# A transformer layer on one core: the last product turned to tokens on the partitions, and the first half's outputs queued behind the last casts

## The chip, the core and the metric

The kernel runs on one core of a Trainium2 chip. Its engines are TensorE (PE, matmuls into the accumulation memory PSUM, with the weight loads shown as PEld), VectorE (DVE), ScalarE (ACT), GpSimd (POOL) and SyncE (SP, which here only issues DMA transfers). Each engine works through its own queue in order, and waits there for results of the others. The metric is the device time of one execution in microseconds (us); a table further down says how the profile's span stands to it.

## What is computed

One layer of a diffusion backbone over 1024 tokens of 1024 features: two attention mixers, then a feed-forward part. Only the end of the layer matters here:

```python
u = h @ w_up                                  # 1024 x 5632
u = conv(u, 3 taps along the tokens) + conv_b
gate, val = jnp.split(u, 2, axis=-1)
y = (jax.nn.silu(gate) * val) @ w_down        # 1024 x 2816 by 2816 x 1024
x = _layer_norm(ALPHA * x + gate2 * y, ln2_g, ln2_b)
```

`gate2` is one number for each feature. The LayerNorm takes the mean and the variance over the 1024 features of a token, and `ln2_g`, `ln2_b` are again one number for each feature. All is in 32-bit floats.

## The kernel before

**Layout.** Until the last stage the features are on the partitions: eight feature tiles f of 128 rows, with the tokens along the free dimension. The tokens are cut into two halves of 512 (h0, h1), and for the last LayerNorm the second half into two quarters (`LN2_S`, line 43: 0 to 512, 512 to 768, 768 to 1024). A scale that is one number for each feature is then one number for each partition, which an instruction takes as a scalar operand.

**Split matmuls.** Each operand is split into a high and a low half (`split`, lines 80 to 87: a cast on ACT gives `hd`, then a subtraction on DVE, line 87, gives `ld`), and a product is three matmuls, high by high, high by low, low by high (`mm3`, lines 89 to 92). So a k-tile of a product can start on PE with `hd` alone and stops at its second matmul where `ld` is not there yet.

**The down projection.** It is done by Strassen's scheme with seven products of half size. In the code's order they are 1, 6, 2, 7, 4, 5 (the loop over `p` at line 1503) and then product 3, which is the last one. Each of the six has 11 k-tiles, with four feature tiles of 512 tokens: 12 matmuls of 512 columns for a k-tile (`product`, line 1465). `dload` (line 1213) loads the two operands of a k-tile by two transfers on SP's queue (lines 1220 and 1221) and splits them; it is called up to three k-tiles ahead (`dnext`), into a ring of four slots (`ring`, line 1150). The operands of product 3 are loaded during products 7, 4 and 5 for the first seven k-tiles (`D3AT`, line 49, each at a fixed place), and behind product 5 for the other four. The results of a product are added onto the residual `zz` by DVE (`accum`, line 1436) while the next product runs.

**Order of the instructions.** The order on PE is the order of the code (line 1177). On the other engines and on SP the scheduler of the framework sets a fixed order when the kernel is built, from readiness and from the order in the code. Work that is to run beside a product is put on a list `pend` with distances; `tick` (line 1004) counts the matmul columns that were issued and emits the next step when its distance is reached, and `drain` emits what is left.

**LayerNorm with features on the partitions** (`ln_steps`, line 1018). Sums and sums of squares over the features come from matmuls with a vector of ones (`stats`), the reciprocal root from a power on POOL (line 1038), diagonal matrices (`diags`) and matmuls with a matrix of ones spread mean and scale over the partitions (`cast`, line 1045), and ACT copies them to `rb` and `mb` (line 1050). Then, for each of the eight feature tiles, `apply` multiplies by `rb` on DVE (line 1055), subtracts `mb` (line 1057, on POOL for all tiles of the first half, on DVE and POOL in turn for the second quarter) and calls `emit2`: an affine function on ACT with the feature's gain and bias (line 1430) and the output's transfer on SP (line 1431). The first half goes this way during product 5, by the distances `LN2_D`.

**Product 3** works on the second half's 512 tokens and gives feature tiles 0 to 3; feature tiles 4 to 7 are complete after product 5. It is done for the third quarter of the tokens first (`r = LN2_S[1]`): matmuls of 256 columns, seven k-tiles for all four feature tiles, then the other four k-tiles for each. The quarter's LayerNorm by `ln_steps`, with the distances `LN2_E`, runs during the product of the last quarter, which has the same form: 4 feature tiles x 11 k-tiles x 3 matmuls of 256 columns.

**The last 256 tokens** are normalized the other way round. `tok(f)` (line 1555) transposes feature tile f of both 128-token tiles by PE into PSUM (`zt`, line 1559), so that tokens are on the partitions and the statistics over the features are one `bn_stats` per 512 features (line 1562). Tiles 4 to 7 are transposed during the product of the third quarter, and tiles 0 to 3 each after its product of the last quarter has been added (`accum`), the last of them after PE's last product. Then DVE subtracts the mean and multiplies by the gain (line 1617), and multiplies by the reciprocal root and adds the bias (line 1607; for the first token tile ACT and POOL do this, lines 1604 and 1605). Four transfers of 256 KB take the result out (line 1610).

Of the kernel before, what the change touches and what calls it, by code (L numbers as in the profile page):

```python
# [13 lines left out]
P = 128  # L14
# [25 lines left out]
LN2_E = 3500.0, 3000.0, 1500.0, 800.0, 500.0  # L40
# [11 lines left out]
OTP = (0, 0), (0, 1)  # L52
OTO = (0, 0), (0, 1), (1, 0), (1, 1)
OTK = 4
OTA = 1
OTB = 2
# [13 lines left out]
def layer_kernel(  # L70
# [8 lines left out]

    def split(src, hi, lo, hi_eng, lo_eng):  # L80
        if hi_eng is nc.scalar:
            nc.scalar.copy(hi, src)  # L82
# [4 lines left out]
        lo_eng.tensor_tensor(out=lo, in0=src, in1=hi.bitcast(F32), op=ALU.subtract)  # L87
# [930 lines left out]
    def ln_steps(zs, zq, s, nm, emit, first, gap, gap1, gap2, each, pm=2, order=range(KT)):  # L1018
# [34 lines left out]
        def apply(f):  # L1053
# [6 lines left out]
        return [(first, stats), (gap, diags), (gap1, cast)] + [(gap2 if n == 0 else each, lambda f=f: apply(f))  # L1060
                                                for n, f in enumerate(order)]
# [400 lines left out]
    d3, evict, after = [], [], []  # L1462
    h0, h1 = hsl(0), hsl(1)

    def product(p):
# [3 lines left out]
        for k in range(NH):  # L1469
# [8 lines left out]
            h, l = dq.pop(0)  # L1478
            for f in range(4):
# [23 lines left out]
    for p in (1, 6, 2, 7, 4, 5):  # L1503
        if p == 6:
# [4 lines left out]
            for a in (0, 1):  # L1509
                nc.sync.dma_start(lnr[a], ln2_row[a].partition_broadcast(P))  # L1510
        if p == 5:
# [35 lines left out]

    s = LN2_S[-1]
    w = s.stop - s.start
    nt = w // P  # L1550
# [4 lines left out]
    def tok(f):  # L1555
        if f % 4 == 0:
            zt[f // 4] = [sml(f"zt{f}_{t}", keep=True) for t in range(nt)]
        for t in range(nt):
            nc.tensor.transpose(zt[f // 4][t][:, (f % 4) * P:(f % 4 + 1) * P],
                                zv(f, slice(s.start + t * P, s.start + (t + 1) * P)), ident)  # L1560
            if f % 4 == 3:
                nc.vector.bn_stats(out=bst[:, t, f // 4], in_=zt[f // 4][t])

    todo = [4, 5, 6, 7]
# [13 lines left out]
    for f in range(4):  # L1578
# [3 lines left out]
        tok(todo.pop(0))  # L1582
    pend += ln_steps(zs2, zq2, r, "b1", emit2, *LN2_E, LN2_P[1])
    r = LN2_S[2]
    for f in range(4):
        o = sml(f"yl{f}_{r.start}")[:, 0:r.stop - r.start]
        last_mm(o, f, r, range(NH))
        accum(f, r, o, True)
        if todo:
            tok(todo.pop(0))  # L1590
        todo.append(f)
    hput(*[f"{a}d3_{k}" for k in range(len(D3AT)) for a in "hl"])
    hfree += xs
    tok(3)
    for t in range(nt):
        nc.vector.bn_aggr(out=mv[:, t], in_=bst[:, t].rearrange("p a b -> p (a b)"))
    nc.vector.tensor_scalar(out=mv[:, :, 1], in0=mv[:, :, 1], scalar1=LN_EPS, scalar2=None, op0=ALU.add)
    nc.gpsimd.tensor_tensor(out=mv[:, :, 1], in0=mv[:, :, 1], in1=mhalf[:, 0:nt], op=ALU.pow)
    ot = {}

    def last(t, a):
        o = ot[t, a]
        if (t, a) in OTP:
            nc.scalar.activation(o, o, AF.Identity, scale=mv[:, t, 1:2])
            nc.gpsimd.tensor_tensor(out=o, in0=o, in1=lnr[1][:, a], op=ALU.add)
        else:
            nc.vector.scalar_tensor_tensor(out=o, in0=o, scalar=mv[:, t, 1:2], in1=lnr[1][:, a],
                                           op0=ALU.mult, op1=ALU.add)
        ts = slice(s.start + t * P, s.start + (t + 1) * P)
        nc.sync.dma_start(out[4 * a:4 * a + 4, :, ts].rearrange("f p q -> p f q"),  # L1610
                          o.rearrange("p (f q) -> p f q", q=P))

    drain(OTK)
    for n in OTO:
        t, a = n
# [123 lines left out]
```

## Time and profile before

| what | us |
|---|---|
| median of three runs | 1586.05 |
| lowest and highest of them | 1584.53, 1586.13 |
| the profiled execution, whole | 1583.75 |
| its span, first to last instruction | 1582.0 |
| PE busy in the span | 1526.0 (96%) |
| DVE busy | 1192.4 (75%) |
| ACT busy | 811.3 (51%) |
| POOL busy | 759.6 (48%) |

All places in time below are microseconds from the span's start in the profiled execution. A row of an engine's timeline gives the start, the duration over all instructions of the row, the engine, the line of the code, the operation, what it writes and reads, the shapes and their number; in brackets stands how long the engine was idle before it and what ended that. A row of a group gives after the bar the busy time and the mean of one in nanoseconds. The mean clock that TensorE was granted over the whole span is 0.995 of full speed.

### The profile page before, as it was taken

To read this page: it belongs to the slowest core of one execution; us is meant where nothing else is said; L and a number is where in the kernel's file an instruction comes from. 1 tells how busy PE (TensorE), PEld (TensorE's weight loads), DVE (VectorE), ACT (ScalarE), POOL (GpSimd) and SP (SyncE) were. 2 spreads that over 40 slices of the span, in tenths; PEclk is the share of its full clock that TensorE was granted. 3 is DMA by queue.
4 is the path that set the end of the run, shared out by engine and by line. 5 is a ranking of instruction groups with operands and counts; after the bars stand their busy time and mean duration, and the time that the engine had idled before them with its cause. 6 is when DMAs were issued, how large, how long until landed. Compare 5 with 4: busy or idle time off the path is not lost.

```text
span 1582.0 us, 22065 instructions
## 1 busy us (share of the span) xinstructions
PE 1526.0 (96%) x7680; PEld 1266.0 (80%) x7680; DVE 1192.4 (75%) x1758; ACT 811.3 (51%) x1441; POOL 759.6 (48%) x738
## 2 busy tenths in 40 slices
PE   6999999999999999999999999999999999999996
PEld 5878788878886887777788898888888888888876
DVE  7797646628887777788674779888888787657885
ACT  5422222448887667688522565444444444435642
POOL 0583302426667556665432554766667664021142
PEclk9999999999999999999999999999999999999998
DMA  9695662322236555532451122333334447996721
GB/s 378 231 321 183 207 214 83 120 81 66 63 99 162 139 126 139 115 84 41 142 174 66 67 95 91 109 107 115 111 107 120 110 113 189 365 267 209 257 94 54
DMA packets 112367, 229.98 MB, mean 145 GB/s; under 512 B 12960, under 2 KB 27808, under 8 KB 112160
## 3 DMA queue, kind: packets, MB, share of 16 engines
q1 hardware_dynamic: 96816, 198.93, 37.9%
q0 software_dynamic: 10400, 20.19, 8.3%
q10 hardware_dynamic: 5040, 9.46, 1.6%
q8 instruction: 60, 0.98, 0.3%
q14 instruction: 51, 0.42, 0.1%
HBM read 177.35 MB, written 65.86 MB: 154 GB/s over the span
## 4 chain that ended last, share of the span: by engine, by line
PE 79%; DVE 9%; ACT 4%; DMA 4%; issue 3%; POOL 2%; SPq 0%; DVEq 0%; ACTq 0%; POOLq 0%
PE ptr L531 5%; PE p L91 4%; PE p L92 4%; PE p L90 4%; PE b L92 3%; PE b L91 3%; PE b L90 3%; PE a L91 2%; PE d L91 2%; PE c L91 2%; PE d L90 2%; PE c L90 2%; PE a L90 2%; PE c L92 2%; PE d L92 2%
## 5 line engine op out<-in xcount | busy, mean ns | idle before, releaser
L541 DVE TENSOR_TENSOR ptl<-ptr,pth 128x512 fp32r<-128x512 f32 x188 | 124.6, 684 | 27.9 <-ACT pth L540 25.5
L531 PE MATMUL ptr<-ident,p 128*128 128x128 f32 x816 | 126.5, 278 | 9.3 <-DVE ptl L541 7.0
L540 ACT CAST pth<-ptr 128x512 fp32r<-128x512 f32 x188 | 106.6, 588 | 56.3 <-PE ptr L531 32.5
L87 DVE TENSOR_TENSOR ld<-rd,hd 128x1024 fp32r<-128x1024 f32 x77 | 95.1, 1253 | 51.0 <-ACT hd L82 48.9
L426 ACT ACTIVATE p<-p,nm 128x1024 f32<-128x1024 f32 (+2 forms) x128 | 125.4, 981 | 11.2 <-DVE p L459 10.4
L531 PEld LDWEIGHTS ptr<-ident,p 128*128 128x128 f32 x816 | 93.7, 140 | 39.5 <-DVE ptl L541 13.7
L82 ACT CAST hd<-rd 128x1024 fp32r<-128x1024 f32 x77 | 79.3, 1050 | 80.4 <-PE p L92 53.2
L91 PE MATMUL p<-ld,hd 128*128 128x512 f32 x264 | 103.8, 393 | 3.7 <-DVE ld L87 3.7
L552 PE MATMUL av<-pth,VT 128*128 128x512 f32 x236 | 104.7, 443 | 1.1 <-ACT avs L558 0.5
L90 PE MATMUL p<-hd 128*128 128x512 f32 x264 | 104.0, 394 | 0.0
L92 PE MATMUL p<-hd,ld 128*128 128x512 f32 x264 | 103.7, 393 | 0.0
L90 PE MATMUL g<-hh,whg 128*128 128x512 f32 x256 | 100.0, 390 | 0.0
L92 PE MATMUL g<-hh,wlg 128*128 128x512 f32 x256 | 99.8, 390 | 0.0
L91 PE MATMUL g<-hl,whg 128*128 128x512 f32 x256 | 99.6, 389 | 0.0
L553 PE MATMUL av<-ptl,VT 128*128 128x512 f32 x236 | 97.6, 414 | 2.0 <-POOL ptl L87 1.8
L87 POOL TENSOR_TENSOR wlg<-wg,whg 128x512 fp32r<-128x512 f32 x32 | 43.3, 1362 | 112.7 <-ACT whg L82 112.7
L459 DVE TENSOR_SCALAR_CACHE_REDUCE p<-s,cvt,nmc 128x1024 f32<-128x1024 f32 x64 | 84.4, 1339 | 12.3 <-PE s L415 12.0
L414 PE MATMUL s<-KL,q 128*128 128x512 f32 (+2 forms) x192 | 76.0, 396 | 2.9 <-ACT p_x L426 2.0
L188 DVE CUSTOM_DVE_ANT_0 wml<-wml,sc,bmc 128x1024 f32<-128x1024 f32 x32 | 46.2, 1456 | 40.6 <-DMA wml<-in_wmodT_dram 40.3
L84 POOL TENSOR_SCALAR pth<-prw 128x512 fp32r<-128x512 f32 x48 | 31.1, 648 | 87.3 <-ACT prw L537 61.8
L82 ACT CAST wS<-s 128x512 fp32r<-128x512 f32 x76 | 45.2, 620 | 53.5 <-POOL s L1079 52.6
L415 PE MATMUL s<-KL,q 128*128 128x512 f32 (+2 forms) x192 | 71.7, 373 | 0.0
(394 smaller groups left out, 4964.2 us busy)
## 6 DMA issues: line engine op xcount, KB each, us to landing
wml<-in_wmodT_dram SPq DMA_DIRECT2D x48, 512.0 KB
ru<-in_w_up_dram SPq DMA_DIRECT2D x38, 512.0 KB
rd<-td SPq DMA_DIRECT2D x55, 256.0 KB
rd<-sd SPq DMA_DIRECT2D x44, 256.0 KB
rd<-in_w_dn_dram SPq DMA_DIRECT2D x33, 256.0 KB
wm<-in_wmodT_dram SPq DMA_DIRECT2D x16, 512.0 KB
wg<-in_w_g_dram SPq DMA_DIRECT2D x32, 256.0 KB
sgd<-sg ACTq DMA_DIRECT2D x32, 256.0 KB
```

The source lines that it names most:

```text
L82: nc.scalar.copy(hi, src)
L87: lo_eng.tensor_tensor(out=lo, in0=src, in1=hi.bitcast(F32), op=ALU.subtract)
L90: nc.tensor.matmul(ps, a[0], b[0], start=start, stop=False, skip_group_check=resumed)
L91: nc.tensor.matmul(ps, a[0], b[1], start=False, stop=False, skip_group_check=resumed)
L92: nc.tensor.matmul(ps, a[1], b[0], start=False, stop=stop, skip_group_check=resumed)
L426: nc.scalar.activation(p, s, AF.Exp, bias=nm[:, h:h + 1], scale=scale, accum_out=sm[:, h:h + 1])
L459: nc.vector.tensor_scalar(out=p, in0=o, scalar1=self.qscale(nqs)[:, hs] if self.br else -1.0, scalar2=self.other[:, hs], op0=ALU.mult, op1 ...
L531: nc.tensor.transpose(tr[:, h * P:(h + 1) * P], self.pslice(h, n), ident)
L540: nc.scalar.copy(hi, tr)
L541: nc.vector.tensor_tensor(out=lo, in0=tr, in1=hi.bitcast(F32), op=ALU.subtract)
L552: nc.tensor.matmul(self.av, v, hi, start=first, stop=False)
L553: nc.tensor.matmul(self.av, v, lo, start=False, stop=self.left == 0)
```

## The change

The code changes in four places.

First, the first half's LayerNorm in product 5. Its last four `apply` (feature tiles 4 to 7) are held on DVE behind `low5`, the low half of the split of product 5's last k-tile. Its eight affine outputs are no longer emitted with each `apply`. They are collected in `outs` and emitted from `tick` during product 3, each held on ACT behind `last_cast`, the last cast of product 3's operands. `issue_after(x)` orders the instructions in its block behind x on x's engine.

Second, the product of the last 256 tokens. The operands change places: 128 tokens are the stationary operand, and the 512 features of the weight the moving one. It has 2 token tiles x 11 k-tiles x 3 matmuls of 512 columns and comes out with the tokens on the partitions. The transposes of feature tiles 0 to 3 no longer wait for it: they are emitted at four fixed k-tiles of the first token tile, and what they transpose is the residual without the product.

Third, the sum behind it. The gate is now one number for each column, so it is needed as a tile `grow` that holds the four feature tiles' (negated) gates on every partition. Two transfers make it, early in product 6: one writes the gates to DRAM, one reads them back spread to 128 partitions. `finish` then does for each token tile by itself, as soon as its product is done: product times gate, plus transposed residual, statistics, and the two operations on each half, all on DVE but the power, with two output transfers of 256 KB. The line that read the output together on the host follows the new layout.

Fourth, the distances `LN2_E` of the second quarter's LayerNorm are new.

```diff
-LN2_E = 3500.0, 3000.0, 1500.0, 800.0, 500.0
+LN2_E = 3500.0, 1500.0, 1500.0, 500.0, 400.0
+OUT_D = 600.0
+TOK_K = 2, 4, 6, 8
...
+        def held(f):
+            with tc.issue_after(behind[0]):
+                apply(f)
+
+        return [(first, stats), (gap, diags), (gap1, cast)] + [
+            (gap2 if n == 0 else each, lambda f=f, fn=held if behind is not None and n >= 4 else apply: fn(f))
+            for n, f in enumerate(order)]
...
             h, l = dq.pop(0)
+            if p == 5 and not dseq and not low5:
+                low5.append(low[0])
...
+    grow = ht("grow", (P, HALF))
+    grd = dpool.tile([4, P], F32, tag="grd", name="grd")
...
+            nc.sync.dma_start(grd.rearrange("f p -> p f"), nmod[:, 0:4])
+            nc.sync.dma_start(grow, grd.rearrange("f p -> (f p)").partition_broadcast(P))
...
-            after.append(lambda: pend.extend(ln_steps(zs2, zq2, h0, "b0", emit2, *LN2_D, LN2_P[0])))
+            after.append(lambda: pend.extend(ln_steps(zs2, zq2, h0, "b0", lambda f, s: outs.append((f, s)), *LN2_D,
+                                                LN2_P[0], behind=low5)))
...
+    last_cast = cast[0]
...
+    drain()
+
+    def late_out(f, s):
+        with tc.issue_after(last_cast):
+            emit2(f, s)
+
+    pend += [(OUT_D, lambda a=a: late_out(*a)) for a in outs]
...
-    r = LN2_S[2]
-    for f in range(4):
-        o = sml(f"yl{f}_{r.start}")[:, 0:r.stop - r.start]
-        last_mm(o, f, r, range(NH))
-        accum(f, r, o, True)
-        if todo:
-            tok(todo.pop(0))
-        todo.append(f)
...
+    def finish(t, y):
+        u.append(ht(f"ut{t}", (P, HALF)))
+        ot.append(ht(f"ot{t}", (P, 2, HALF)))
+        m, rs = mv[:, t, 0:1], mv[:, t, 1:2]
+        nc.vector.tensor_tensor(out=u[t], in0=y, in1=grow, op=ALU.mult)
+        nc.vector.tensor_tensor(out=u[t], in0=u[t], in1=zt[0][t], op=ALU.add)
+        nc.vector.bn_stats(out=bst[:, t, 0], in_=u[t])
+        nc.vector.bn_aggr(out=mv[:, t], in_=bst[:, t].rearrange("p a b -> p (a b)"))
+        nc.vector.tensor_scalar(out=rs, in0=rs, scalar1=LN_EPS, scalar2=None, op0=ALU.add)
+        nc.gpsimd.tensor_tensor(out=rs, in0=rs, in1=mhalf[:, 0:1], op=ALU.pow)
+        for a in (1, 0):
+            nc.vector.scalar_tensor_tensor(out=ot[t][:, a], in0=(u[t], zt[1][t])[a], scalar=m, in1=lnr[0][:, a],
+                                           op0=ALU.subtract, op1=ALU.mult)
+        for a in (1, 0):
+            o = ot[t][:, a]
+            nc.vector.scalar_tensor_tensor(out=o, in0=o, scalar=rs, in1=lnr[1][:, a], op0=ALU.mult, op1=ALU.add)
+            nc.sync.dma_start(out[4 * t + 2 * a:4 * t + 2 * a + 2, :, s].rearrange("f p q -> p f q"),
+                              o.rearrange("p (f q) -> p f q", f=2))
+
+    for t in range(nt):
+        q = slice(s.start - HALF + t * P, s.start - HALF + (t + 1) * P)
+        y = sml(f"yt{t}")
+        for k in range(NH):
+            h, l = d3[k]
+            mm3(y, (h[:, 1, q], l[:, 1, q]), (h[:, 0], l[:, 0]), k == 0, k == NH - 1)
+            tick(HALF / 0.8)
+            if t == 0 and k in TOK_K:
+                tok(TOK_K.index(k))
+        finish(t, y)
```

More of the change, by code (lines that the diff above doesn't have):

```diff
@@ L1016, in drain, with ln_steps @@
             clock[0] = 0.0
-    def ln_steps(zs, zq, s, nm, emit, first, gap, gap1, gap2, each, pm=2, order=range(KT)):
+    def ln_steps(zs, zq, s, nm, emit, first, gap, gap1, gap2, each, pm=2, order=range(KT), behind=None):
         w = s.stop - s.start
@@ L1461, in layer_kernel @@
     nside = [0]
-    d3, evict, after = [], [], []
+    d3, evict, after, outs, low5 = [], [], [], [], []
     h0, h1 = hsl(0), hsl(1)
@@ L1581, in layer_kernel @@
         sums(f, r, False)
[L1582 removed]
+        tok(4 + f)
     pend += ln_steps(zs2, zq2, r, "b1", emit2, *LN2_E, LN2_P[1])
[L1584 to L1596 removed]
@@ L1597, in layer_kernel @@
[L1597 to L1611, printed above, removed]
@@ L1613, in layer_kernel @@
[L1613 to L1622 removed]
+    hfree += xs
+    u, ot = [], []
+    def finish(t, y):
[16 more added lines that the diff above has]
+                              o.rearrange("p (f q) -> p f q", f=2))
```

29 lines of the change are left out of this document (7 added, 22 removed).

## The prediction

> **What bounds the kernel now.** I read the page first, for the bound of the whole.
>
> ```profile
> span 1582.0 us, 22065 instructions
> PE   6999999999999999999999999999999999999996
> ```
>
> TensorE (PE) is full in every slice but the first and the last. So a change at the end is worth only what it takes out of PE's line of work there, plus what it takes out of the stretch after PE's last matmul. Next the busy time by stage, with cuts at the places where PE stops or changes pace (columns: stage, its length, busy time of PE, PEld, DVE, ACT, POOL, the granted clock, DMA share, GB/s), and PE's waits from 1300 us on.
>
> ```profile
> 1525.04:1528.93 3.89, 0.17 (x2) 0.01 (x1) 3.83 (x2) 1.88 (x3) 3.89 (x3) 0.87 0.39 146
> 1528.93:1533.78 4.85, 4.85 (x11) 3.84 (x12) 1.96 (x2) 3.64 (x4) 1.07 (x1) 0.50 0.30 110
> 1533.78:1534.82 1.04, 1.04 (x7) 1.03 (x6) 1.04 (x2) 0.80 (x1) 0.00 (x0) 0.53 0.00 0
> 1534.82:1550.83 16.01, 16.01 (x138) 16.01 (x136) 11.15 (x19) 3.18 (x8) 5.79 (x7) 1.00 0.00 1
> 1550.83:1569.07 18.24, 18.24 (x153) 18.11 (x151) 10.10 (x26) 5.10 (x11) 4.80 (x6) 1.00 0.12 41
> 1569.07:1582.00 12.93, 0.66 (x4) 0.20 (x2) 7.91 (x12) 1.77 (x3) 3.63 (x3) 0.62 0.37 106
> ```
>
> ```profile
> PE p L91 <- DVE ld L87: 3.7, 1, 3.7
> ```
>
> Three things are to be seen. PE stands still once, before 1528.93, in the last k-tile of product 5, for the low half `ld` of a split. The next 4.85 us run at clock 0.50. And 12.93 us lie behind the last product. Why `ld` is late stands in the order of DVE and ACT:
>
> ```profile
> 1515.20 11.46 DVE L1055 TENSOR_TENSOR zz<-zz,rbb 128x512 f32<-128x512 f32 x8 [0.53 <-ACT rbb L1050]
> 1526.59 2.28 DVE L87 TENSOR_TENSOR ld<-rd,hd 128x1024 fp32r<-128x1024 f32 x1
> L1437 DVE SCALAR_TENSOR_TENSOR zz<-p,nmod,zz 128x512 f32<-128x512 f32 x12 | 8.7, 741 | 1.1 <-PE p L92 1.1
> L87 DVE TENSOR_TENSOR ld<-rd,hd 128x1024 fp32r<-128x1024 f32 x77 | 95.1, 1253 | 51.0 <-ACT hd L82 48.9
> 1512.36 1.06 ACT L82 CAST hd<-rd 128x1024 fp32r<-128x1024 f32 x1 [1.70 <-PE p L92]
> 1521.08 0.82 ACT L1430 ACTIVATE of<-zz,ln2c 128x512 f32<-128x512 f32 x1 [0.88 <-POOL zz L1057]
> 1521.80 1.04 ACT L82 CAST hd<-rd 128x1024 fp32r<-128x1024 f32 x1
> ```
>
> All eight LayerNorm multiplications of the first half (L1055) stand ahead of the split of the last k-tile on DVE (the next two rows are means, of an addition and of a split), and three affine outputs (L1430), each waiting for a subtraction on POOL, ahead of its cast on ACT. The pace of PE, one row each side of the stall and two of the 256-column product:
>
> ```profile
> 1524.59 0.39 PE L92 MATMUL p<-hd,ld 128*128 128x512 f32 x1
> 1524.81 0.39 PE L90 MATMUL p<-hd 128*128 128x512 f32 x1
> 1530.37 0.63 PE L91 MATMUL p<-ld,hd 128*128 128x512 f32 x1
> 1530.80 0.63 PE L92 MATMUL p<-hd,ld 128*128 128x512 f32 x1
> 1542.84 0.28 PE L90 MATMUL yl<-hd 128*128 128x256 f32 x1
> 1542.96 0.28 PE L91 MATMUL yl<-ld,hd 128*128 128x256 f32 x1
> ```
>
> Start to start, a 512-column matmul costs 0.227 us (rounded rows: 0.22), 0.43 behind the stall, and a 256-column one 0.12.
>
> **Part 1: the order in product 5.** The last four multiplications are held behind the split of the last k-tile, and all eight affines go behind the last cast. With no affine ahead of it the cast waits only for its slot. PE frees one each 2.72 us (12 x 0.227), and the cast before it ran at 1512.36, so this one starts near 1516. DVE does four multiplications, 4 x 1.43 = 5.7 us, to 1520.9, then the split, 2.3 us at worst: 1523.2. PE asks at 1525.04, so 1.8 us are to spare and the stall goes. Without it the eleven matmuls end at 1525.04 + 11 x 0.227 = 1527.53 in place of 1533.78, which is **-6.25 us**, and the slow start of the next product goes too, 1.04 us in place of some 0.65: **-0.4**.
>
> What is late next? DVE still owes four multiplications (5.7 us), four splits for product 3 (about 5 us) and, once product 5 ends, eight additions and three sums of squares, some 6.7 us: from 1523.2 that makes about 1540.6. PE meets the first of these, four transposed tiles, only behind 96 matmuls x 0.12 = 11.5 us, at 1539.0. So a wait of 0 to 2 us is possible there; I take **+0.3**, as most of these tiles are done in order and the first is needed first. The eight affines are 8 x 0.82 = 6.6 us of ACT; the window from 1534.82 to 1550.83 has ACT busy 3.18 of 16.01, so they cost nothing there. Without that cover they would cost at most 6.6. Their eight transfers meet an idle DMA (share 0.00). The SP queue has no loads left behind them.
>
> [...] The trace has 3.7 us of idle PE and then 4.85 us at clock 0.50. [...]
>
> **Part 2: the last product.** Before, 4 feature tiles x 33 matmuls of 256 columns: 132 x 0.12 = 15.84 of the 18.24 us; the other 2.40 are statistics, broadcasts and transposes. Now 2 token tiles x 33 of 512 columns: 66 x 0.227 = 14.98, plus 2.40 and one more pair of transposes (0.22): 17.6, which is **-0.6 us**. PE ends at 1550.83 - 6.65 + 0.3 + 17.6 = 1562.1. The second token tile starts one broadcast (about 0.85 us) and 33 matmuls (7.5) before, so the first ends at 1553.75.
>
> Both tiles take the same PSUM bank, since the rotating list has come round. The second therefore waits for the first DVE operation of the first (0.7 us); the broadcasts on PE (0.85 us) cover that, so I cost it at nothing. If that operation stood behind the eight multiplications of the second quarter, it would cost what the second rival says.
>
> **Part 3: DVE after the first token tile.** The work is new here; nearest rows:
>
> ```profile
> L1376 DVE TENSOR_TENSOR pv<-b,pv 128x512 f32<-128x512 f32 x13 | 8.8, 677 | 0.0
> L1562 DVE BATCH_NORM_STATS2 bst<-zt 128x6 f32<-128x512 f32 x4 | 2.6, 687 | 0.4 <-PE zt L1559 0.4
> L1617 DVE SCALAR_TENSOR_TENSOR ot<-zt,bmv,lnr 128x512 f32<-128x512 f32 x4 | 2.8, 742 | 0.0
> 1562.04 0.76 DVE L1055 TENSOR_TENSOR zz<-zz,rbb 128x256 f32<-128x256 f32 x2 [1.65 <-ACT rbb L1050]
> 1566.16 0.47 DVE L1437 SCALAR_TENSOR_TENSOR zz<-yl,nmod,zz 128x256 f32<-128x256 f32 x1
> 1567.37 0.41 DVE L1057 TENSOR_TENSOR zz<-zz,mbb 128x256 f32<-128x256 f32 x1
> L1057 POOL TENSOR_TENSOR zz<-zz,mbb 128x256 f32<-128x256 f32 x4 | 3.3, 837 | 7.8 <-DVE zz L1055 7.8
> 1572.19 0.16 DVE L1597 TENSOR_SCALAR bmv<-bmv 128x2 f32<-128x2 f32 x1
> 1572.42 0.70 POOL L1598 TENSOR_TENSOR bmv<-bmv,mhalf 128x2 f32<-128x2 f32 x1 [4.04 <-DVE bmv L1597]
> 1573.71 0.52 issue
> ```
>
> Per token tile: two 128x512 operations, statistics, aggregate and epsilon, 0.65 + 0.65 + 0.62 + 0.2 + 0.2 = 2.3 us at their spacing, then four scalar_tensor_tensor of 0.66: 5.0 us. The second quarter's LayerNorm, now due later in the product, takes 1562.04 to 1567.78 less one 0.47 us addition: 5.3 us. From 1553.75 DVE has 5.0 + 5.3 us before it can turn to the second tile: 1564.1, two us after PE has ended. So **DVE, not PE, sets the end**, whichever of the two goes first, since both must be done. The second tile takes 5.0 us (the power of POOL, 0.70 plus 0.23 to reach it, lies beside two operations of 1.3), and 0.5 for the unexplained issue time seen before: 1569.6. An operation with two inputs beside a busy POOL could take twice as long (the rows of Part 4), at most 3.3 us for POOL's four subtractions, and these are inside the 5.3.
>
> **Part 4: the last transfers.** Before:
>
> ```profile
> 1574.23 3.21 DVE L1607 SCALAR_TENSOR_TENSOR ot<-ot,bmv,lnr 128x512 f32<-128x512 f32 x2
> 1575.25 3.20 SPq L1610 DMA_DIRECT2D out_dram<-ot  x4
> DMA packets 2112, 1.05 MB, mean 131 GB/s; under 512 B 64, under 2 KB 2112, under 8 KB 2112
> ```
>
> The last DVE operation ends at 1577.44 and the span at 1582.0, 4.56 us later. Four outputs of 256 KB went out in one rush; now two do, the other two having gone 5 us earlier. A transfer takes about 0.9 us (1.05 MB at some 290 GB/s), so between 0 and 0.9 us of queueing goes; I take 0.5, which leaves 4.1. The two operations of 3.21 us ran beside POOL at 1.6 us each; they are 0.66 now, which the sum above has.
>
> **Sum.** 1569.6 + 4.1 = 1573.7, against 1582.0: **-8.3 us**. The profiled execution took 1583.75 us, 1.75 outside the span; the median of the three runs is 2.3 above it, 1586.05. Off the median: **1577.8 us**.
>
> **Part 5: the gate's spread.** Early, in product 6, the SP queue gets two more transfers: 512 gate values of 4 bytes to DRAM, and their broadcast to 128 partitions, which waits for the first to land. Behind it stand the loads of product 6:
>
> ```profile
> 1358.49 2.63 SPq L1510 DMA_DIRECT2D lnr<-in_ln_row_dram x2
> 1362.88 0.33 SPq L1220 DMA_DIRECT2D rd<-sd  x1
> 1371.79 1.05 ACT L82 CAST hd<-rd 128x1024 fp32r<-128x1024 f32 x1 [1.67 <-PE p L92]
> SPq L506 <- DMA dn<-rb: 6.5, 10, 1.1
> td<-tg POOLq DMA_DIRECT2D x1, 512.0 KB, 9.6
> ```
>
> The load of 1362.88 is for the cast of 1371.79, which PE itself released: 8.9 us. The ring has four slots, so from the cast to the use lie three k-tiles, 8.2 us, of which cast and split take 2.3; that leaves 5.9 more. The same kind of round trip through DRAM held SP 0.65 us in the mean (6.5 us in ten waits) with an idle DMA; with the DMA full, a transfer needed 9.6 us to land. Between these bounds nothing reaches PE, so I cost it at nothing. [...]
>
> **The rivals.**
> 1. *The split stays late* (the four held multiplications move, but DVE or ACT still reaches the split near 1526.6). Then 6.65 us of the gain are missing: -1.7, **1584.4**. For it: what orders DVE was not the order of the code, which has the split between the third and fourth multiplication. Against: four of the eight are now bound behind it, and the cast loses its predecessors.
> 2. *The second token tile waits for its bank* behind the eight multiplications on DVE: 1.0 + 5.3 + 0.7 - 0.85 = 6.2 us of idle PE, then 2.4 to 2.8 of slow clock, against 2 us that DVE no longer holds up the end: 8.3 - 6.9 = -1.4, **1584.6**. Against: the bank's reader has its data a microsecond before they have theirs.
> 3. *A smaller gain*: PE waits 2 us for the transposes at 1539 and the transfers save nothing: -8.3 + 1.7 + 0.5 = -6.1, or two us more where DVE's operations run beside POOL; **1580 to 1582**.
> 4. *Slower*: the gate's first transfer holds SP in product 6. It decides where the hold passes 8.9 + 5.9, less one or two for the late load's own landing: about 13 us. Beyond that each microsecond stops PE, and a stall of 3.7 us or more pays another 2.75 for the clock (6.25 + 0.4 - 3.9). With a hold of 24 us: 11 + 2.75 - 8.3 = +5.4, **1591.5**; it is slower at all from 19 us on. Against: 9.6 us is the longest landing seen.
>
> **How the numbers follow.** My forecast 0.62, the first rival 0.10, the second 0.06, the third 0.15, the fourth 0.07. A measurement here tells about 0.2% (3.2 us) from no change, so faster is under 1582.9: 0.62 + 0.15 and a little of the first two, 0.79; the same 0.14; slower 0.07. The forecast's own range is 1575 (no queueing, no idle issue, no wait for the transposes, and one us less of DVE) to 1580. For 8 in 10 it takes the third rival in, and part of the first two: **1574 to 1584**.
>
> **What would show it.** The wait of PE for `ld` in product 5 gone and the clock 1.00 from 1500 to the end of PE; `ld` of the last k-tile on DVE between the fourth and fifth multiplication; the first product of the rest near 1527.5; the transposed second half as 66 matmuls at 0.227; PE's last matmul near 1562; DVE busy without a gap from there to 1569. It is wrong if PE stops anew (transposes near 1539, start of the second token tile, product 6), or if DVE is idle after PE's end, when the tail would be a chain and not a queue.

## The result and the profile after

| | median us | lowest to highest | runs | ratio to before, 95% interval |
|---|---|---|---|---|
| before, first set | 1586.09 | 1584.53 to 1588.47 | 6 | |
| changed | 1579.84 | 1575.00 to 1580.51 | 6 | 0.9953 [0.9938, 0.9968] |
| changed again, beside other kernels | 1577.42 | 1575.15 to 1579.14 | 6 | 0.9944 [0.9927, 0.9960] |

The change takes 0.5% off the time, 7 to 9 us by the two ratios. One of the six executions of one version further down (e10) took 1692.11 us at a clock of 0.85, another state of the chip, and is left out of its numbers. The changed kernel's profiled execution took 1580.51 us, with a span of 1578.6 and a mean clock of 0.994. Line numbers of the changed kernel differ a little from those of before: the lower half of a split is L86, the multiplication by the scale L1054, the subtraction of the mean L1056, the additions onto the residual L1441.

First PE's waits from 1300 us on (total, times, longest):

```profile
PE zt L1578 <- DVE zz L1441: 0.3, 1, 0.3
PE p L90 <- DVE ld L86: 0.3, 1, 0.3
PE stb L1031 <- DVE zq L998: 0.2, 1, 0.2
```

The wait of 3.7 us is gone, and three of 0.2 to 0.3 us are there in its place. (The one for `ld` is another, at 1508.8 us, several k-tiles ahead of the old one.) Next the busy time by stage, with cuts that answer to those of before: product 5 to its end, product 3 with features on the partitions, the turned product, and what lies behind PE's last matmul.

```profile
1521.00:1528.90 7.90, 7.90 (x36) 6.44 (x35) 7.86 (x6) 3.47 (x5) 6.95 (x4) 1.00 0.00 0
1528.90:1533.40 4.50, 4.50 (x22) 3.72 (x21) 4.50 (x4) 1.35 (x2) 3.87 (x4) 1.00 0.00 0
1533.40:1549.60 16.20, 15.75 (x130) 15.36 (x129) 15.29 (x19) 8.59 (x15) 8.94 (x8) 1.00 0.35 126
1549.60:1569.10 19.50, 19.49 (x99) 15.82 (x98) 12.98 (x32) 3.08 (x7) 6.00 (x7) 1.00 0.14 45
1569.10:1578.60 9.50, 0.00 (x0) 0.00 (x0) 5.84 (x12) 3.06 (x6) 3.31 (x4) 0.61 0.42 138
```

PE is busy to the end of product 5 at a clock of 1.00, where before it stood still and then ran at 0.50. The stretch behind the last matmul has shrunk from 12.93 to 9.50 us. ACT has taken the late affines into the third stretch (8.59 of 16.20, before 3.18 of 16.01). The orders on DVE and ACT, from the two timelines:

```profile
1521.04 4.70 DVE L1054 TENSOR_TENSOR zz<-zz,rbb 128x512 f32<-128x512 f32 x4 [0.53 <-ACT rbb L1049]
1525.67 2.32 DVE L86 TENSOR_TENSOR ld<-rd,hd 128x1024 fp32r<-128x1024 f32 x1
1527.91 5.78 DVE L1054 TENSOR_TENSOR zz<-zz,rbb 128x512 f32<-128x512 f32 x4
```

```profile
1522.67 1.05 ACT L81 CAST hd<-rd 128x1024 fp32r<-128x1024 f32 x1 [0.80 <-PE p L91]
...
1540.97 0.80 ACT L1434 ACTIVATE of<-zz,ln2c 128x512 f32<-128x512 f32 x1
```

The split of the last k-tile stands between the fourth and the fifth multiplication, its cast has no affine ahead of it, and the first affine comes 18 us behind that cast.

**Where the time came from.** The matmuls of product 5 and product 3 are the same instructions in both kernels until the turned product, so each can be set against itself. Rows of PE after:

```profile
1530.65 0.39 PE L89 MATMUL p<-hd 128*128 128x512 f32 x1
...
1533.37 0.28 PE L89 MATMUL yl<-hd 128*128 128x256 f32 x1
...
1533.85 0.28 PE L90 MATMUL yl<-ld,hd 128*128 128x256 f32 x1
...
1545.83 0.33 PE L1578 MATMUL zt<-ident,zz 128*128 128x128 f32 x1 [0.33 <-DVE zz L1441]
...
1550.86 0.48 PE L89 MATMUL yt<-hd 128*128 128x512 f32 x1
1551.18 0.40 PE L90 MATMUL yt<-ld,hd 128*128 128x512 f32 x1
...
1568.70 0.39 PE L91 MATMUL yt<-hd,ld 128*128 128x512 f32 x1
```

The matmul ahead of the old stall ran at 1524.81 before and at 1530.65 now, 5.84 late. The first of product 3 ran at 1533.78 and now at 1533.37, 0.41 early. A further 0.4 comes in that product's first microsecond, as its matmuls are 0.12 apart from the start. At the transposes it gives back 0.85 and reaches the turned product at 1550.86, where the old last product began at 1550.83. PE's last matmul ends at 1568.70 + 0.39 = 1569.09, just where the last product ended before (1569.07). The rest is the stretch behind it, 3.4 us shorter: 0.6 ahead of DVE's last two operations (5.16 us before, from 1569.07 to 1574.23, and 4.58 now, to 1573.67), 1.8 in these two (3.21 us beside POOL before, 1.41 now) and 1.0 in the last transfers (4.56 and 3.52). From the old stall on, then, 5.84 + 3.4 = 9.2 us were gained.

The 5.84 us by which this execution came late to the old stall lie outside the change's place. Up to the last k-tiles of product 5, PE, DVE, ACT and POOL have the same instructions in the same order in both kernels, and 3.2 us of the delay are there before the first transfer of the gate, at 825 us, is issued: a matmul that starts at 819.65 before starts at 822.88 here. Six windows show most of the delay:

```profile
96.70:100.10 3.40, 1.10 (x4) 0.36 (x2) 3.40 (x5) 2.75 (x5) 3.32 (x3) 1.00 0.99 383
100.10:103.50 3.40, 2.81 (x7) 2.23 (x8) 3.40 (x7) 0.00 (x0) 2.54 (x3) 0.51 0.91 317
786.20:789.60 3.40, 1.68 (x7) 0.86 (x5) 3.03 (x4) 1.08 (x2) 0.47 (x1) 1.00 0.64 169
789.60:793.00 3.40, 3.33 (x8) 2.65 (x9) 3.12 (x3) 0.91 (x1) 1.21 (x2) 0.50 0.36 144
1509.80:1513.20 3.40, 3.17 (x22) 2.82 (x22) 3.30 (x4) 0.94 (x1) 0.09 (x1) 1.00 0.43 152
1513.30:1516.70 3.40, 3.40 (x10) 2.63 (x9) 2.19 (x7) 1.04 (x1) 1.03 (x1) 0.50 0.85 245
```

They are three pairs: a stretch in which PE streams few columns (4 and 7 matmul records in the first two; in the third it is busy, but 16 of its 22 records are one column wide), then 3.4 us at a clock of 0.50 or 0.51, which loses about 1.7 us (an estimate, 3.4 x 0.5). The profiled execution of before had none of these short drops. They come and go between executions of one kernel: in the first set the changed kernel's times follow the mean clock, 1575.00 us at 0.998, 1578.50 at 0.996, 1580.51 at 0.994. They are not all, since in the second set times from 1575.61 to 1579.14 stand at the same 0.997. The profile of before, at 1583.75 us, is below all six times of its set, and all eleven profiles of the versions with the change or a part of it reach this place later than it, by 0.9 to 5.8 us.

### The profile page after: what moved, and what is told of

Same layout as the page of the kernel before. It is cut to its first block, busy times and chain, and to the rows that moved or that the text cites. A ratio compares the mean times of both kernels' runs of the same rounds, so it can differ in the third digit from the quotient of the medians.

```text
span 1578.6 us, 21930 instructions
## 1 busy us (share of the span) xinstructions
PE 1528.4 (97%) x7614; PEld 1264.6 (80%) x7614; DVE 1198.0 (76%) x1761; ACT 808.9 (51%) x1439; POOL 756.5 (48%) x737
## 2 busy tenths in 40 slices
DMA packets 112015, 230.25 MB, mean 146 GB/s; under 512 B 13504, under 2 KB 27328, under 8 KB 111808
## 4 chain that ended last, share of the span: by engine, by line
PE 73%; DVE 12%; DMA 5%; ACT 4%; issue 3%; POOL 1%; SPq 0%; ACTq 0%; DVEq 0%; POOLq 0%
PE ptr L530 5%; PE b L91 3%; PE b L90 3%; PE b L89 3%; PE g L89 3%; PE g L91 3%; PE g L90 3%; PE s L413 2%; PE av L551 2%; PE c L90 2%; PE d L90 2%; PE a L90 2%; PE c L89 2%; PE d L89 2%; PE a L89 2%
## 5 line engine op out<-in xcount | busy, mean ns | idle before, releaser
L86 DVE TENSOR_TENSOR ld<-rd,hd 128x1024 fp32r<-128x1024 f32 x77 | 97.6, 1284 | 50.8 <-ACT hd L81 48.7
L425 ACT ACTIVATE p<-p,nm 128x1024 f32<-128x1024 f32 (+2 forms) x128 | 125.3, 981 | 11.1 <-DVE p L458 10.3
L86 POOL TENSOR_TENSOR wlg<-wg,whg 128x512 fp32r<-128x512 f32 x32 | 44.2, 1388 | 112.7 <-ACT whg L81 109.2
L81 ACT CAST wS<-s 128x512 fp32r<-128x512 f32 x76 | 45.3, 621 | 51.0 <-POOL s L1083 50.2
```

The lines of the kernel that those rows point to most:

```text
L81: cast[:] = [nc.scalar.copy(hi, src).ins]
L86: low[:] = [lo_eng.tensor_tensor(out=lo, in0=src, in1=hi.bitcast(F32), op=ALU.subtract).ins]
L425: nc.scalar.activation(p, s, AF.Exp, bias=nm[:, h:h + 1], scale=scale, accum_out=sm[:, h:h + 1])
```

## The experiments

**Each half of the change by itself.** The kernel before with part 1 alone, and the changed kernel without it:

```diff
 e1: before, with
+            with tc.issue_after(behind[0]):   # the last four apply
+                apply(f)
...
+        with tc.issue_after(last_cast):       # the eight affines
+            emit2(f, s)
```

> The kernel before with part 1 alone: the first half's last four tokens tiles of applies held behind the fifth lower part, its affines queued behind the last cast; the last product, the tail and the last loads stay those of before. My theory (the stall of PE for ld in product 5 is the order of DVE's and ACT's queues, and its price is idle time plus the half clock): the wait of 3.7 us for ld is gone, the first product of the rest starts about 6.7 us earlier against its neighbours, the tail stays at 12.9 us from PE's last matmul to the end, and the time falls by about 6 us, ratio near 0.996. Rival (the gain comes from the last product alone, and the order only moves the wait elsewhere): a wait of 3 us or more appears at the transposes or in product 6, and the ratio is 0.999 to 1.001.

```diff
 e2: changed, with
-            after.append(... lambda f, s: outs.append((f, s)), *LN2_D, LN2_P[0], behind=low5)))
+            after.append(... emit2, *LN2_D, LN2_P[0])))
```

> The changed kernel without part 1: the first half's applies and affines as before, the last product with tokens on the partitions kept. My theory: the stall for ld comes back (3.7 us and half a clock window, 6 to 7 us in all), the tail from PE's last matmul to the end keeps the 9.5 us that the changed kernel showed against 12.9 before, and the time is 3 to 4 us under the kernel before, ratio near 0.998; this and the run with the order alone add up to 9 to 10 us, more than the change's measured 7.4, the rest being short clock drops outside the change. Rival (the last product's new form is worth nothing, since DVE queues after it): ratio 0.999 to 1.001.

The order alone gave 1581.22 us, ratio 0.9963 [0.9951, 0.9975]; the turned product alone 1583.50 us, 0.9982 [0.9971, 0.9993]. Together that is 0.55%, and the whole change has 0.47 to 0.56%: within the intervals the two parts add up. PE's waits from 1300 us on and the stages of the order alone:

```profile
PE zt L1579 <- DVE zz L1445: 0.7, 2, 0.4
```

```profile
1524.00:1533.80 9.80, 9.80 (x47) 8.19 (x46) 9.80 (x7) 3.17 (x3) 9.17 (x6) 1.00 0.00 0
1569.00:1582.00 13.00, 0.70 (x5) 0.22 (x3) 7.91 (x12) 1.81 (x3) 3.63 (x3) 0.72 0.38 106
```

and of the turned product alone:

```profile
PE p L90 <- DVE ld L86: 3.7, 1, 3.7
```

```profile
1532.30:1537.20 4.90, 4.89 (x12) 3.83 (x13) 2.00 (x2) 3.64 (x4) 1.09 (x1) 0.50 0.29 107
1572.13:1581.70 9.57, 0.00 (x0) 0.00 (x0) 5.90 (x12) 3.06 (x6) 3.37 (x4) 0.65 0.42 137
```

The first has no stall and the old tail of 13 us; the second has the stall, the half clock and the new tail of 9.57. Neither rival holds. The second run takes the turned product, the new sum behind it and the distances as one. Whether the product had to be turned for the 1.8 us and the 1.0 us of the tail, or whether DVE alone for the last operations and earlier transfers would have given them, was not run.

**Is half of the stall's price the clock?** Sixteen matmuls into a bank that nobody reads, where PE waits:

```diff
 e7: before, at product 5's last k-tile, first feature tile
+                    nc.tensor.matmul(acc[f], h[:, 0, c], h[:, 1], start=False, stop=False)
+                    for _ in range(16):
+                        nc.tensor.matmul(fill, h[:, 0, c], h[:, 1], start=True, stop=True)
...
```

> The kernel before, with 16 more matmuls of 128x512 (3.6 us at 0.227) into a bank that nobody reads, put on PE where it waits 3.7 us for ld. They do no work of the reference. Theory A (the stall is half idle time and half clock: PE idle for a window costs the next two at half speed): the first product of the rest starts no earlier, but the 30 or so matmuls behind it run at 0.227 in place of 0.43, the clock stays 1.00 there, and the time falls by 2.5 to 3.4 us, ratio near 0.998. Theory B (the slow matmuls behind the stall come from the operands or the banks, not from the clock): they stay slow and the ratio is 0.999 to 1.001.

It took 1583.65 us, 0.9987 [0.9977, 0.9997], which is 2.1 us with an interval of 0.5 to 3.6. PE's timeline there (the profiled execution was the slowest of the twelve, 1588.12 us):

```profile
1531.99 3.79 PE L1485 MATMUL fill<-hd 128*128 128x512 f32 x16
1535.93 0.50 PE L1486 MATMUL p<-ld,hd 128*128 128x512 f32 x1 [0.15 <-DVE ld L87]
...
1538.56 0.28 PE L90 MATMUL yl<-hd 128*128 128x256 f32 x1
```

and the window of the eleven matmuls behind the gap:

```profile
1535.93:1538.56 2.63, 2.63 (x11) 2.17 (x12) 0.00 (x0) 1.51 (x2) 1.09 (x1) 1.00 0.28 103
```

The real work starts no earlier, but the eleven matmuls take 2.63 us at clock 1.00, in place of 4.85 at 0.50. Theory A holds, a little below its numbers (2.1 us by the ratio, 2.5 to 3.4 expected). Matmuls without any use made the kernel faster. So of the stall's 6.65 us 3.9 were idle time and, by the rows, 2.75 the clock.

**Which of part 1's two edits is it?** Part 1 holds four multiplications on DVE, and it puts the affines off on ACT. The hold alone:

```diff
 e3: changed, with
-            after.append(... lambda f, s: outs.append((f, s)), *LN2_D, LN2_P[0], behind=low5)))
+            after.append(... emit2, *LN2_D, LN2_P[0], behind=low5)))
```

> The changed kernel with the last four applies held behind the fifth lower part, but the first half's affines emitted at once, ahead of the last cast on ACT. My theory (the hold alone does it; the cast then waits for three affines and the lower part is done near 1525 in before's time, as PE comes to it): a wait of PE for ld of at most 0.5 us, and the changed kernel's time within 0.1%. Rival (the late affines are needed as well): the cast moves behind more affines, 2 to 4 us of the stall and half a clock window come back, and the time is 3 to 6 us over the changed kernel's.

and the late affines alone:

```diff
 e4: changed, with
-                                                LN2_P[0], behind=low5)))
+                                                LN2_P[0])))
```

> The changed kernel with the late affines but without the hold on the last four applies, so that nothing but the place of the affines differs from the run without part 1. My theory (the stall is DVE's order: the lower part of the last k tile stands behind all eight multiplications unless the last four are held): the wait of PE for ld and the half clock behind it come back in part, at least 2 us of idle, and the time is 2 to 4.5 us over the changed kernel's, about that of the run without part 1. Rival (the affines on ACT, ahead of the cast, were what kept the lower part late): no wait for ld over 0.5 us, and the changed kernel's time within 0.1%.

The hold alone took 1580.21 us, 0.9963 [0.9946, 0.9981], where the changed kernel beside it had 1577.42, 0.9944 [0.9927, 0.9960]. The intervals overlap, and the profile has to tell. Its waits, the place on PE, and two windows:

```profile
PE zt L1578 <- DVE zz L1441: 2.3, 2, 2.2
```

```profile
1542.33 0.48 PE L1578 MATMUL zt<-ident,zz 128*128 128x128 f32 x1 [2.15 <-DVE zz L1441]
```

```profile
1539.40:1542.80 3.40, 1.25 (x7) 0.72 (x6) 3.40 (x7) 0.83 (x2) 2.36 (x3) 0.91 0.00 0
1542.80:1546.20 3.40, 3.22 (x19) 3.21 (x19) 2.86 (x7) 0.42 (x1) 0.73 (x1) 0.59 0.00 0
```

The stall for `ld` is gone, as my theory said, but from product 3's first matmul to the end of the span this profile has 48.5 us (from 1528.42 to 1577.0), and both of the changed kernel have 45.3 (from 1533.37 to 1578.6 and from 1531.99 to 1577.3). The rival had the size (3 us or so) and the wrong place: with the affines ahead of them, ACT's casts for product 3 come late, DVE's splits and additions behind them too, and PE waits 2.15 us for the transposes and then has a clock of 0.59 over the next 3.40 us.

The late affines alone took 1578.12 us, 0.9952 [0.9938, 0.9967]: as fast as the whole change, and its profile has no wait of PE after 1300 us. From product 3's first matmul to the end it has 45.5 us (from 1529.58 to 1575.0): PE comes through product 3 some 0.9 us sooner, but DVE does not, and the stretch behind PE's last matmul is 10.6 us. Here my theory fell and the rival held. The order on DVE, from its timeline:

```profile
1517.52 3.10 DVE L1054 TENSOR_TENSOR zz<-zz,rbb 128x512 f32<-128x512 f32 x5
1520.53 1.22 DVE L86 TENSOR_TENSOR ld<-rd,hd 128x1024 fp32r<-128x1024 f32 x1
1521.67 1.89 DVE L1054 TENSOR_TENSOR zz<-zz,rbb 128x512 f32<-128x512 f32 x3
```

Nothing holds the multiplications here, and yet the last three stand behind the split. The order on DVE is fixed when the kernel is built, from readiness and the code's order; as I read the rows, with the affines out of ACT's way the cast comes early, and the split took its place without a hold.

**The gate's spread.** The gate's row loaded from the gain's row, in one transfer (so the output has the gain where the gate belongs):

```diff
 e5: changed, with
-            nc.sync.dma_start(grd.rearrange("f p -> p f"), nmod[:, 0:4])
-            nc.sync.dma_start(grow, grd.rearrange("f p -> (f p)").partition_broadcast(P))
+            nc.sync.dma_start(grow, ln2_row[0, 0].partition_broadcast(P))
```

> The changed kernel with the gate row loaded from the norm's gain row in one transfer, so without the spread of the gate through DRAM (the output has that row in place of the gate). My theory (the spread is issued at 825 us and holds nothing that anyone waits for): the same time within 0.2%, 1575 to 1581 us by the number of clock drops, and d3's late landing in product 5 either recurs or is chance. Rival (the 512 descriptors of the one-element transfer hold the queue that loads d3, so that products 5 and 6 start later): d3's casts 2 to 3 us earlier against PE, the two short waits of PE at 1505 and at the statistics (0.5 us together) gone, and 1.5 to 3 us less.

It took 1576.61 us, 0.9941 [0.9928, 0.9954], beside 0.9953 and 0.9944 of the changed kernel: no difference that can be measured. Its profile lacks the two short waits of product 5, but so does the second profile of the changed kernel, so they were chance. The two transfers in the changed kernel's timeline of SP:

```profile
825.44 0.39 SPq L1519 DMA_DIRECT2D grd<-nmod  x1
...
1365.26 0.33 SPq L1520 DMA_DIRECT2D grow<-grd  x1
```

The first is issued 540 us ahead of the second, so that nothing waits for its landing.

**The changed kernel again,** as a base:

> The changed kernel itself again, beside the next three on one chip, as their base. My theory: its times spread over 1575 to 1581 us by the number of clock windows at half speed (1.7 us each, on a grid of 3.413 us), with 1573.5 to 1575 us for a run without one; ratio to the kernel before 0.994 to 0.996. Rival (the 5 us that its first profiled execution carried into product 5 belong to the change): the same three short drops at 100, 790 and 1513 us in the profile again.

1577.42 us, 0.9944 [0.9927, 0.9960]. Of the waits after 1300 us only that at the transposes is left (0.3 us). Its mean clock is 0.997, and its one short drop lies at 170 us, none at 100, 790 or 1513. Still it is 4.5 us late at product 3 (first matmul at 1531.99, where the profile of before without its stall gives 1527.53), and 4.1 of them are there at 820 us. A part is a wait of PE for a split ahead of that drop:

```profile
170.62 0.79 PE L90 MATMUL accqb<-wlqb,hh 128*128 128x512 f32 x1 [3.65 <-DVE wlqb L86]
```

So the 5.84 us carried in the first profile are not drops of the clock alone, and the early part of them is not the change's; where the rest of the second profile's delay comes from was not traced.

**Is DVE a queue behind PE's end?**

```diff
 e6: changed, with
-LN2_E = 3500.0, 1500.0, 1500.0, 500.0, 400.0
+LN2_E = 3000.0, 1000.0, 1500.0, 300.0, 400.0
...
+        if t:
+            banks.append(banks.pop(0))
```

> The changed kernel with the last norm's steps due earlier (its cast after 1000 in place of 1500, its applies after 300 in place of 500) and the second token tile in a fresh bank. My theory (behind PE's end DVE is the queue: it has the applies of the last norm still to do, so the last finish starts 0.7 us after PE's end): the applies end about 1.4 us earlier, the second finish starts with PE's last matmul, the 0.3 us wait for the bank goes, and the time falls by 0.7 to 1.3 us. Rival (the tail is a chain of waits between DVE and GpSimd and not a queue): 0 to 0.3 us less.

1576.49 us, 0.9937 [0.9924, 0.9949]. In the changed kernel the second token tile's work on DVE begins at 1569.83, right behind the second quarter's last subtraction and 0.7 us after PE's end (the first row is the first token tile's):

```profile
1560.53 0.69 DVE L1608 TENSOR_TENSOR ut<-yt,grow 128x512 f32<-128x512 f32 x1 [1.80 <-PE yt L91]
...
1569.49 0.42 DVE L1056 TENSOR_TENSOR zz<-zz,mbb 128x256 f32<-128x256 f32 x1
1569.83 0.68 DVE L1608 TENSOR_TENSOR ut<-yt,grow 128x512 f32<-128x512 f32 x1
...
1573.67 1.41 DVE L1619 SCALAR_TENSOR_TENSOR ot<-ot,bmv,lnr 128x512 f32<-128x512 f32 x2
```

With the earlier steps it begins with PE's end (1565.35 + 0.39 = 1565.74), and what is behind that end is 8.86 us:

```profile
1547.78 0.48 PE L89 MATMUL yt<-hd 128*128 128x512 f32 x1
...
1565.35 0.39 PE L91 MATMUL yt<-hd,ld 128*128 128x512 f32 x1
```

```profile
1565.84 0.69 DVE L1608 TENSOR_TENSOR ut<-yt,grow 128x512 f32<-128x512 f32 x1
```

```profile
1565.74:1574.60 8.86, 0.00 (x1) 0.00 (x0) 5.19 (x10) 1.01 (x2) 1.28 (x2) 0.63 0.41 137
```

The wait for the bank is gone too. So the queue was real and worth 0.6 us, and the bank 0.3: from product 3's first matmul to the end it is 44.4 us (from 1530.27 to 1574.6), where the changed kernel has 45.3. The intervals of the two times overlap, and only the profile shows it.

**Can the short drops of the clock be kept off?** The two norms of 512 tokens have eight one-column matmuls (sixteen records) in a row for their statistics. In the changed kernel's first profile the drop at 1513 us came behind these, and in e6 the 512-column matmuls near them (864 to 874 us) took 0.434 to 0.445 us in the mean, against 0.39 in rows at a clock of 1.00.

```diff
 e8: e6, with
-        return [(first, stats), (gap, diags), (gap1, cast)] + [
+        if n == 4:
+            head = [(first, lambda: stats(0, 1))] + [(SPLIT, lambda t=t: stats(t, t + 1)) for t in (1, 2, 3)] + [
+                (gap - 2 * SPLIT, diags)]
...
```

> The version with the last norm's steps due earlier, and its two 512-token norms' one-column statistics matmuls dealt out by token tile, three matmuls of a product between each pair, in place of eight in a row. My theory (a window of 3.413 us in which PE streams fewer than some 0.38 of its columns puts the next at half clock, and eight one-column matmuls with the short waits around them make such a window by chance of phase): no half window near 870 and 1513 us, and 0.5 to 1.5 us less on the median than with the statistics in a row, so 1575.0 to 1576.0 us, ratio near 0.993. Rival (the drops come from something else): a half window near 870 us again in half of the profiles, and no gain, or a loss of up to 1 us from the norm's later end.

1575.85 us, 0.9936 [0.9921, 0.9952], and its profile has a mean clock of 0.999, without a drop before PE's end. Then both together, without the hold, and the same with the statistics in a row:

```diff
 e9: e8, and e10: e6, both with
-                                                LN2_P[0], behind=low5)))
+                                                LN2_P[0])))
```

> The version with the last norm's steps due earlier and the statistics dealt out, and without the hold on the last four applies, as the run with the late affines alone had no wait of PE behind 1300 us. My theory (the late affines do all of part 1 and the hold only costs 0.8 us at the transposes): no wait of PE over 0.2 us from 1300 us on, no half window near 870 and 1513 us, and 1574 to 1575.5 us, ratio near 0.9925. Rival (the hold is worth something when the statistics come later): a wait for ld of 0.5 us or more, and 1576 us or over.

> The same as the other kernel of this call, with the statistics in a row as in the changed kernel. My theory (eight one-column matmuls in a row make a half window by chance of phase near 870 us in half of the executions, 1.7 us each): a mean granted clock lower by 0.001 to 0.002 over the runs and 0.5 to 1.5 us more than the other. Rival (no such effect): the same time and the same clocks.

They took 1577.26 us, 0.9941 [0.9929, 0.9953], and 1575.91 us (the median of five), 0.9937 [0.9922, 0.9951]. Both missed: e10 was to be the slower one, e9 was to come to 1574 to 1575.5, and both e8 and e9 have a wait of 0.8 us at the transposes; the hold's price of 0.8 us that I took from the late affines alone is not there either, since e10 waits 0.3 us at the transposes as the changed kernel does. The pairs settle what the hold is worth beside the late affines. e6 and e10 differ by it alone, and both take 44.4 us from product 3's first matmul to the end (e10 from 1533.32 to 1577.7); e8 and e9 differ by it alone, and both take 45.0 (from 1528.84 to 1573.8 and from 1532.28 to 1577.3). It is worth nothing either way. What the run with the late affines alone had of its own is told in the last section. As to the clock, from 1505 to 1545 us the second matmuls of product 5's k-tiles (`p<-ld,hd`) took 0.389 us in the mean in e8 and e9, 0.409 in e10 and 0.413 in the changed kernel's first profile, which has its drop at 1513 there; but c_after, e1 and e3 to e6, with the statistics in a row, have 0.389 or 0.390 too, and the times of e9 and e10 differ by less than their spread. That dealing the statistics out saves time is not shown.

None of the versions is measurably faster than the changed kernel; e6, e8 and e10 have the lowest medians, by 1 to 1.5 us.

## Why the prediction was right, point by point

The forecast of 1577.8 us lies between the two medians of 1579.84 and 1577.42. Its sum of -8.3 stands against -9.2 from the old stall on. That the sum came within 1 us is in part luck: PE ended 1.15 us later than the sum had it (1563.25 in before's time, for 1562.1), and the tail was 2.1 us shorter. The terms:

1. *The stall and the slow start, -6.25 and -0.4.* Measured -6.25 (from +5.84 to -0.41) and -0.4. Right. The mechanism was right only in part: holding the last four multiplications was taken for the cure, but the late affines do it without the hold (e4, e9 and e10), and the hold alone pays elsewhere (e3). The remark under the first rival, that DVE's order is not the code's, was nearer to it than the step itself.
2. *The wait at the transposes, +0.3 in 0 to 2.* Measured +0.85, inside. The affines' 6.6 us of ACT, costed at nothing, are hidden where they were put; the hold alone shows their price where they stay early, 2.15 us of wait and a drop of the clock.
3. *The last product, -0.6.* This step failed: it is 0.0 (18.23 us from its first matmul to its last one's end, before 18.24). About half is the bank, which I costed at nothing because the broadcasts would cover it. Those who waited for DVE's first operation on the first token tile:

```profile
  PEld yt L89: 0.3, 1
```

With a fresh bank (e6) the product took 1565.74 - 1547.78 = 17.96 us. The rest stands in single rows: seven 512-column matmuls behind transposes, statistics or broadcasts take 0.31 to 0.34 in place of 0.227, as from 1550.86 to 1551.18 above, some 0.6 us in all. The sum had all 66 at 0.227, and the neighbours themselves some 0.3 us too long.

4. *DVE behind the first token tile: free 2 us after PE's end, then 5.5.* DVE, not PE, set the end, as forecast, but by 0.7 us and not 2: the two pieces that I put at 10.3 us took 9.3 (1560.53 to 1569.83), and PE ended later. The second tile took 5.25, where the sum had 5.5.
5. *The last transfers, 4.1.* Measured 3.5 (from 1573.67 + 1.41 = 1575.08 to the span's end at 1578.6), 0.1 us beyond the better bound. Terms 4 and 5 together made the tail 11.6; it is 9.5. This is the term that was furthest off.
6. *The gate's spread at nothing.* Right (e5), though not for the reason given: I had both transfers at the start of product 6, and the scheduler issued the first at 825 us. The fourth rival lost its premise with that.
7. *Off the median.* Adding the term to the median was right, and it hid how the single executions stand: the profile of before had no short drop of the clock, the first one of the changed kernel three. So the clock was not 1.00 from 1500 us to PE's end there, as it was to be: one drop lies at 1513.

The first rival (the split stays late) and the fourth (SP held) did not come. Of the second 0.3 us came, of 6, and of the third the transposes, with 0.85 of 2.

By the rows above, the clock fell behind stretches in which PE was not idle throughout: in the hold alone PE was busy 1.25 of 3.40 us ahead of 3.40 us at a mean of 0.59, and in the changed kernel 3.17 of 3.40 us ahead of 3.40 us at 0.50, where 16 of the 22 matmul records are one column wide.

The changed kernel moves 112015 packets in its span and the one without the spread (e5) 111487. The 528 more are all under 512 bytes (13504 against 12976), for 512 gate values; what the other 16 are was not traced. They cost no time that can be measured, since nobody waited for them.

## What to carry to other kernels

When an engine waits late for a small piece of work, ask which queue that piece stands in first: here the place of eight outputs on ACT decided the order on DVE two steps on, and moving them was enough. Here PE's stall of 3.7 us, with 6.83 us at a clock of 0.50 from 1527.92 us on, was worth 6.65 us; a few dummy matmuls tell the idle time and the clock apart. Behind the last product, add up what every engine still owes at that moment, other stages' leftovers included.

## What the runs showed of the hardware

**In two profiles the granted clock changed on a grid of 3.413 us.** By the clock records of the profile of before, the drop at the old stall lasts 6.827 us, from 1527.92 us on, at 0.50; in those of the changed kernel's first profile the three drops before PE's end last 3.413 us each, from 100.14, 789.63 and 1513.26 us on, at 0.50. All starts lie whole steps of 3.413 us behind the first stretch at 1.00 (443 steps for the old stall's, 24, 226 and 438 for the others). Ahead of each drop PE streamed few columns. Counted at 0.443 ns for a column (0.227 us / 512, an estimate, and some matmul records can be missing), the step ahead of the old stall's drop came to 0.15 of its length, those ahead of the three short ones to 0.19, 0.37 and 0.35. Steps of 0.41 (at 667.8 us, before) and of 0.45 and 0.35 (at 735.0 and 670.2 us, changed kernel) had no drop behind them, so this estimate gives no sharp bound, and the 0.38 of the theory ahead of e8 is no more than such an estimate. At 100, 790 and 1513 us the changed kernel had drops in its first profile and none in its second. That the place of the grid decides whether a thin stretch brings a drop is my reading; no run varied it.

**DVE and POOL took different times beside each other.** In product 5 DVE multiplies and POOL subtracts, each with two inputs. In the run with the late affines alone:

```profile
L1056 POOL TENSOR_TENSOR zz<-zz,mbb 128x512 f32<-128x512 f32 x8 | 19.6, 2488 | 4.4 <-DVE zz L1054 4.4
L1054 DVE TENSOR_TENSOR zz<-zz,rbb 128x512 f32<-128x512 f32 x8 | 5.0, 688 | 0.0
```

and in the changed kernel, with the same instructions:

```profile
L1056 POOL TENSOR_TENSOR zz<-zz,mbb 128x512 f32<-128x512 f32 x8 | 14.5, 1841 | 6.3 <-ACT mbb L1049 5.7 <-DVE zz L1054 0.6
L1054 DVE TENSOR_TENSOR zz<-zz,rbb 128x512 f32<-128x512 f32 x8 | 10.5, 1368 | 0.5 <-ACT rbb L1049 0.5
```

One of DVE's took 688 ns and one of POOL's 2488 in the first, 1368 and 1841 in the second. In the first POOL's eight subtractions lasted 19.60 us, from 1518.35, and DVE's eight multiplications, with a split between, had ended by 1523.56. All other profiles are like the second (DVE 1368 to 1505 ns, POOL 1772 to 1843), but for the hold alone, which has DVE at 962 ns and POOL at 1769. This one instance is why the late affines alone had no wait at the transposes, as far as the profile tells; what decides which way it goes is open.
